# Output projection on scaled fp16 weight parts, in one pipeline with the feed-forward stage

## The chip, the core and the metric

The kernel runs on one core of a Trainium2 chip. The metric is the device time of one execution in microseconds; lower is better. The engines of the core are named as in the profile: PE (TensorE, matmuls) with PEld (its weight loads), DVE (VectorE), ACT (ScalarE), POOL (GpSimd) and SP (SyncE, which here only issues DMAs).

## What is computed

One step of a decoder layer for 288 token rows: a prompt of 256 tokens and 8 samples of 4 tokens each. All inputs are fp32. The parts that matter here are the end of the mixer, the output projection and the feed-forward network:

```
mod = silu(c) @ w_ada + b_ada                  # sh1, sc1, gt1, sh2, sc2, gt2, 2048 each
gate   = sigmoid(mg).reshape(B, T, 3, 2048)    # mg is a part of xn @ w_in
merged = gate[:, :, 0] * (y_lru @ w_br_lru) + gate[:, :, 1] * (y_gla @ w_br_gla) + gate[:, :, 2] * (y_ml @ w_br_ml)
x  = x + gt1 * (merged @ w_out)                # w_out 2048 x 2048
xn = rmsnorm(x, g_norm2) * (1.0 + sc2) + sh2
x  = x + gt2 * (square(relu(xn @ w_ff1)) @ w_ff2)   # w_ff1 2048 x 8192
y  = rmsnorm(x, g_final)
```

Everything before `merged` (three recurrent branches and their states) is computed by the kernel as well and is the same on both sides of the change.

## The kernel before

Activations lie with features on the 128 partitions and the 288 tokens along the free axis; a row of 2048 features is 16 such tiles, called k = 0 to 15 below. Weights stream from memory in tiles of 128 x 1024 values (0.5 MB). To keep fp32 accuracy each weight and each activation is split into a high and a low part, and each product is three matmuls: high by high, high by low, low by high. A step is one weight tile: 24 matmuls of 128 x 128 by 288.

There are two such streams. `stream` (L152) does the input projection, the gates, the branch projections and the output projection: ACT writes the high part of a tile as fp32r (L160), DVE the low part (L162), and the matmuls follow at L169. It has three buffers each for the raw tile, the high and the low part. The feed-forward stage uses `Block` (L226): it first finds a power of two for the whole block of four tiles (`scan`, a sum of squares on ACT, L236; `total`, one small matmul with a tile of ones, L240; `scale`, a few one-column DVE operations, L195), and then splits the scaled tile into fp16 parts (`convert`, L249 on ACT or L251 on DVE for the high part, L252 on DVE for the low part). The matmuls are at L263. `feed_forward` (L1956) is a list of 256 steps; in step s it converts tile s + 3, fetches tile s + 14, scans tile s + 10 and multiplies tile s. A block of w_ff1 is 256 columns wide with four k in a tile, a block of w_ff2 512 columns with two k in a tile.

Order is set in four ways. Under `in_order` (L207) the instructions of PE, ACT and DVE are issued as they stand in the program. `tc.issue_after` ties single instructions behind another. The rest of PE, ACT, DVE and POOL is ordered by the compiler's scheduler, with `tc.high_priority` for hints. SP alone issues strictly in the program's order, and a DMA whose target is still in use holds all those behind it.

Beside the main stream runs the conditioning product (mod). Its weights come in loads of 1 MB. A string of letters after `every(` says what is done after each step: L loads one unit, V multiplies all loaded units, F four of them, C advances the splitting of a unit that is multiplied in fp16 parts (`cond_parts`, L403; its matmuls are at L433), and a dot does nothing. Units without parts (`cond_product`, L355) are multiplied in plain fp32 at L372. The order of the units is fixed in `units` (L527). The second half of SC2 (the units sm1) is multiplied in parts beside the output projection; the eight units of the first half of GT2 (gt0) are loaded then too and are multiplied at its end.

Around the change the work runs like this. `merge` (L1295) is called for each of the three branches; for each of four blocks of 512 columns it runs eight steps of a gate block (w_in), then four steps of the branch block. In the third call POOL adds the last term (L1330) and ACT and DVE split the merged rows into fp32r parts (L1333, L1334), which lie in slots 0 to 3. Slots are ten buffers of 128 x 8 x 288 fp32 that are used in turn. The gates read the normalised input from two larger tiles, xh and xl, which are free after the last gate block. The output projection (L1780 on) is 4 blocks of 8 steps with `ev_o` as eviction: residual (`resid`, L1763), squares for the norm (`sumsq`, L593). In its last block the rows are scaled by SC2 on POOL (`scaled`, L1773). After it come the row sums with ones (L608), the root (`rstd_of`, L636), and `second_norm` (L1815), which makes the fp16 parts of the normalised row k: a product by the root (L1820, DVE, or POOL for every fourth k), the high part with the shift on ACT (L1821, the samples at L1824), the low part on DVE (L1825, samples L1826). The first four feed-forward steps each begin with four of these, and their matmuls go through the k one by one.

## Time and profile before

| | us |
|---|---|
| median of 3 runs | 1898.62 |
| lowest, highest run | 1896.01, 1898.95 |
| the profiled execution, whole | 1895.68 |
| its span in the profile | 1893.9 |
| granted clock over the span | 0.995 |

A line of a timeline has the start and length in us, the engine, the line of the kernel, the operation, what it writes and reads, and in brackets how long the engine sat idle before it and what ended that. A line by stretch has, after the stretch and its length, the busy time and the number of instructions of PE, PEld, DVE, ACT and POOL, the granted clock of PE, the busy share of the DMA engines and the rate. A line of waits has the waiting engine and its line, the engine and line that ended the wait, the total in us, how often, and the longest. Ends of matmuls are modelled, so their pace is read from starts and counts.

### The profile page before, as it was taken

To read this page: it belongs to the slowest core of one execution; us is meant where nothing else is said; L and a number is where in the kernel's file an instruction comes from. 1 tells how busy PE (TensorE), PEld (TensorE's weight loads), DVE (VectorE), ACT (ScalarE), POOL (GpSimd) and SP (SyncE) were. 2 spreads that over 40 slices of the span, in tenths; PEclk is the share of its full clock that TensorE was granted. 3 is DMA by queue.
4 is the path that set the end of the run, shared out by engine and by line. 5 is a ranking of instruction groups with operands and counts; after the bars stand their busy time and mean duration, and the time that the engine had idled before them with its cause. 6 is when DMAs were issued, how large, how long until landed. Compare 5 with 4: busy or idle time off the path is not lost.

```text
span 1893.9 us, 38893 instructions
## 1 busy us (share of the span) xinstructions
PE 1847.8 (98%) x15874; PEld 1621.6 (86%) x15874; DVE 1268.2 (67%) x2239; ACT 1117.3 (59%) x1861; POOL 219.9 (12%) x302
## 2 busy tenths in 40 slices
PE   8999999999999999999999979999999999999997
PEld 7998889999999999999999947777777777777775
DVE  4767846645684557776558678776868676767676
ACT  5333374545454444566448568877777766666673
POOL 0001200000123010011101520000000000000091
PEclk9999999999999999999999999999999999999999
DMA  9998666547844358856787656565556555556541
GB/s 384 398 372 301 242 236 240 201 145 260 276 159 168 134 172 296 302 204 223 296 341 298 246 210 222 172 222 185 189 188 203 176 181 168 188 169 188 168 155 51
DMA packets 113442, 422.90 MB, mean 223 GB/s; under 512 B 11808, under 2 KB 12096, under 8 KB 110064
## 3 DMA queue, kind: packets, MB, share of 16 engines
q1 hardware_dynamic: 97040, 361.04, 54.9%
q0 software_dynamic: 11472, 42.79, 6.4%
q10 hardware_dynamic: 4752, 16.60, 2.2%
q8 instruction: 124, 2.03, 0.4%
q14 instruction: 54, 0.44, 0.1%
HBM read 403.56 MB, written 16.81 MB: 222 GB/s over the span
## 4 chain that ended last, share of the span: by engine, by line
PE 80%; DVE 9%; ACT 6%; issue 3%; DMA 1%; POOL 0%; SPq 0%; DVEq 0%; ACTq 0%; POOLq 0%
PE mm L169 39%; PE mm L263 24%; PE pi L263 6%; PE pa L372 3%; DVE pair L252 2%; ACT pair L249 2%; PE px L169 2%; DVE lo L162 1%; ACT con L236 1%; DMA raw<-win 1%; ACT hi L160 1%; PE pa L433 1%; DVE pair L251 0%; DVE s L800 0%; PE px L1649 0%
## 5 line engine op out<-in xcount | busy, mean ns | idle before, releaser
L263 PEld LDWEIGHTS <-pair 128*128 128x128 f16 x6144 | 596.6, 98 | 176.8 <-issue 11.9
L160 ACT ACTIVATE hi<-raw 128x1024 fp32r<-128x1024 f32 x272 | 286.9, 1057 | 407.4 <-PE mm L169 250.4
L162 DVE TENSOR_TENSOR lo<-raw,hi 128x1024 fp32r<-128x1024 f32 x272 | 334.9, 1233 | 248.0 <-ACT hi L160 227.9
L169 PE MATMUL mm<-xh,hi 128*128 128x288 f32 x1440 | 429.4, 301 | 4.0 <-ACT xh L718 1.7
L169 PE MATMUL mm<-xl,hi 128*128 128x288 f32 x1440 | 423.5, 297 | 0.0
L169 PE MATMUL mm<-xh,lo 128*128 128x288 f32 x1440 | 411.9, 296 | 2.0 <-DVE lo L162 1.9
L263 PE MATMUL mm<-x,pair 128*128 128x288 f16 x2448 | 316.1, 287 | 10.1 <-ACT x L1824 6.3
L263 PE MATMUL mm<-hx,pair 128*128 128x288 f16 x2472 | 321.8, 286 | 2.7 <-ACT s L1873 1.4
L169 PEld LDWEIGHTS mm<-xh,hi 128*128 128x128 f32 x1440 | 270.4, 188 | 15.8 <-issue 8.1
L169 PEld LDWEIGHTS mm<-xl,hi 128*128 128x128 f32 x1440 | 270.8, 188 | 1.4
L169 PEld LDWEIGHTS mm<-xh,lo 128*128 128x128 f32 x1440 | 266.0, 188 | 4.9 <-DVE lo L162 2.9
L169 PE MATMUL mm<-s,hi 128*128 128x288 f32 x1280 | 252.8, 297 | 1.1 <-DVE s L1769 0.7
L169 PEld LDWEIGHTS mm<-s,hi 128*128 128x128 f32 x1280 | 201.8, 188 | 5.1 <-issue 2.9
L169 PE MATMUL mm<-s,lo 128*128 128x288 f32 x640 | 179.2, 296 | 1.6 <-DVE lo L162 1.0
L252 DVE SCALAR_TENSOR_TENSOR pair<-xl,sums,pair 128x1024 f16<-128x1024 f32 x92 | 117.8, 1284 | 62.9 <-ACT pair L249 61.6
L252 DVE SCALAR_TENSOR_TENSOR pair<-s,sums,pair 128x1024 f16<-128x1024 f32 x92 | 118.1, 1284 | 52.7 <-ACT pair L249 51.4
L252 DVE SCALAR_TENSOR_TENSOR pair<-raw,sums,pair 128x1024 f16<-128x1024 f32 x72 | 93.2, 1295 | 41.6 <-ACT pair L249 40.6
L169 PEld LDWEIGHTS mm<-s,lo 128*128 128x128 f32 x640 | 116.9, 188 | 2.3 <-DVE lo L162 2.1
L1861 POOL TENSOR_SCALAR s<-s,mod 128x256 f32<-128x256 f32 x16 | 21.5, 1347 | 675.7 <-DVE s L1877 675.7
L236 ACT ACTIVATE con<-s 128x1024 bf16<-128x1024 f32 x92 | 96.3, 1046 | 1.3 <-DMA s<-wf 0.3
L236 ACT ACTIVATE con<-xl 128x1024 bf16<-128x1024 f32 x92 | 96.2, 1046 | 0.9
L263 PE MATMUL pi<-hx,pair 128*128 128x288 f16 x600 | 89.8, 286 | 3.1 <-DVE rs_t L1767 1.8
(526 smaller groups left out, 2275.7 us busy)
## 6 DMA issues: line engine op xcount, KB each, us to landing
raw<-win SPq DMA_DIRECT2D x192, 512.0 KB, 4.4
s<-wf SPq DMA_DIRECT2D x92, 512.0 KB, 3.9
xl<-wf SPq DMA_DIRECT2D x92, 512.0 KB, 4.1
raw<-wf SPq DMA_DIRECT2D x72, 512.0 KB, 3.9
s<-wq SPq DMA_DIRECT2D x20, 1024.0 KB, 8.7
raw<-wout SPq DMA_DIRECT2D x32, 512.0 KB, 5.9
s<-wada SPq DMA_DIRECT2D x13, 1024.0 KB, 7.3
ag<-wada POOLq DMA_DIRECT2D x12, 1024.0 KB, 7.8
```

Of the source, the lines that this page charges most:

```text
L160: pace["hi"] = S.activation(hi, raw, AF.Copy)
L162: pace["lo"] = V.tensor_tensor(out=lo, in0=raw, in1=hi.bitcast(F32), op=ALU.subtract)
L169: pace["last"] = T.matmul(ps, w[:, kk, ms], x, start=k == k0 and i == 0, stop=k == kt - 1 and i == 2)
L236: pace["hi"] = S.activation(junk, raw, AF.Square, accum_out=self.of[:, g:g + 1])
L249: pace["hi"] = S.activation(hi, raw, AF.Copy, scale=self.u)
L252: pace["lo"] = V.scalar_tensor_tensor(lo, raw, self.u, hi, ALU.mult, ALU.subtract)
L263: pace["last"] = T.matmul(self.ps[m][:, :N], a[:, kk, m * P:(m + 1) * P], x, start=k == 0 and i == 0, stop=k == 4 * self.kg - 1 and i == 2)
L372: pace["prod"] = T.matmul(ps[32 * j:32 * j + 32, h * w // 4:(h + 1) * w // 4], stat(k), v[:, j], start=k == 0 and h == 0, stop=k == kt - 1 ...
L433: pace["prod"] = T.matmul(ps[32 * j:32 * j + 32, a:a + 256], c, v[:, j], start=q == i == n == 0, stop=q == KT // each - 1 and n == 1, skip ...
L1861: G.tensor_scalar(a[:, 0:NP], a[:, 0:NP], mod[:, GT2, k, 0:1], None, ALU.mult)
```

## The change

The output projection leaves `stream` and becomes eight `Block`s of 256 columns (w_out is packed for that width) at the front of one list with the feed-forward blocks. The list is driven by `feed`, and a record `pipe` holds the state: which tiles are fetched, scanned, converted. A tile is fetched as soon as a place is free, scanned two steps after its fetch at the earliest and up to 12 ahead, and converted up to 5 ahead.

The merged rows become fp16 parts as well. Their power of two must be known before the last rows are there, so it is taken from a bound: the squares of the sums so far, of the last branch weights (`weigh`) and of the norm's weights (`whole_bound`). `halve_merged` then writes the parts, k 0 to 3 in the last branch block and 4 to 15 ahead of the first three projection steps.

The ramp of the pipeline lies in the last part of the third `merge` call. Behind the first step of its third branch block six tiles of w_out are fetched into slots 2, 3 and 5 (`fetch_first`); they are scanned in the last gate block (`gate_then`). Behind the first step of the last branch block four more are fetched into xl, and behind that block three into the raw buffers.

The first two feed-forward blocks are joint: a step takes tile g of both, 48 matmuls, and each of the four steps begins with four `second_norm`s. The units sm1 are no longer in parts; the letter W multiplies one unit. The row sums for the norm are all made at the last k.

The diff, cut to its core:

```diff
+            if on_raw:
+                on_raw(g, flat(raw))
...
+            if then:
+                then(g)
             yield
...
+    def pipe_scan(to):
+        while pipe["scanned"] <= to and pipe["when"].get(pipe["scanned"], pipe["time"]) <= pipe["time"] - 2:
+            i = pipe["scanned"]
+            pipe["blocks"][i // 4].scan(i % 4, pipe["raws"][i])
...
+    def nth(n):
+        j = n - pipe["joint"]
+        return pipe["joint"] + j // 2 + 4 * (j % 2) if 0 <= j < 8 else n
+
+    def pipe_convert(to, rate=2):
+        pipe_scale()
+        for n in range(pipe["converted"], min(to + 1, pipe["converted"] + rate)):
+            i = nth(n)
+            if i // 4 >= pipe["scaled"]:
+                break
...
+            t = wp.tile([P, 2048], F16, tag=("hi", "lo")[n % 2], name=nm("pair"), bufs=3)
...
+            if all(raw is not o for o in pipe["once"]):
+                pipe["places"].append(raw)
+            pipe["converted"] += 1
+            pipe_fetch()
...
+    def feed(count, act, evac, back, factor=1.0, joint=False, late=False):
+        if joint:
+            s = pipe["at"]
+            two = pipe["blocks"][s // 4:s // 4 + 2]
+            for g in range(4):
+                pipe["time"] += 2
+                with in_order():
+                    with ahead():
+                        for f in pipe["before"].pop(s + g, ()):
+                            f()
+                        for b in two if g == 0 else ():
+                            b.start(act, back() if callable(back) else back, factor)
+                        pipe_convert(s + 2 * g + 5)
+                        pipe_scan(s + min(2 * g + 12, 15))
+                    for kk in range(two[0].kg):
+                        for i, b in enumerate(two):
+                            b.multiply(g, *pipe["pairs"][s + 4 * i + g], range(b.nm_t), (kk,))
...
-            yield from ada_half(f"sm{h}", SC2, h, h == 1)
+            yield from ada_half(f"sm{h}", SC2, h)
...
+    pipe["blocks"] += [Block(io["wout"], i, 256) for i in range(8)]
+    for hb in range(9):
+        if hb < 8:
+            pipe["blocks"] += [Block(io["wf1"], 4 * hb + i, 256, by_act=(0,)) for i in range(4)]
+        if hb:
+            pipe["blocks"] += [Block(io["wf2"], i, 512, g0=4 * (hb - 1), by_act=(0, 2, 3)) for i in range(4)]
...
+    def fetch_first():
+        once = [v for i in (2, 3, 5) for v in views(flat(slot(i)))]
+        pipe["once"] = once
+        pipe["places"] += once
+        pipe["time"] += 1
+        with behind_last():
+            pipe_fetch()
...
+    def whole_bound():
+        p = rows_total(zof, 14)
+        for a, b, o in ((0, 8, 14), (8, 12, 15), (12, 14, 4)):
+            V.tensor_reduce(out=zof[:, o:o + 1], in_=p[:, a:b], axis=AX.X, op=ALU.add)
...
+        roots_of(zof)
+        for k in range(4):
+            halve_merged(k)
+
+    def halve_merged(k):
+        m, a, u = mrg[k // 8], acc[k // 8][:, k % 8, :], zof[:, 6:7]
+        S.activation(m[:, 0, k % 8], a, AF.Copy, scale=u)
+        V.scalar_tensor_tensor(m[:, 1, k % 8], a, u, m[:, 0, k % 8], ALU.mult, ALU.subtract)
+
+    def outs_then(g):
+        pipe["time"] += 1
+        with behind_last():
+            if g == 0:
+                bigx.append(flat(big.tile([P, KT, N], F32, tag="xl", name=nm("xl"))))
+                pipe["places"] += views(bigx[0], 4)
+                pipe_fetch()
...
-            run(stream(w, b, lambda k: (y[0][:, k, :], y[1][:, k, :]), 8, ev))
+            ramp = {"on_raw": weigh, "then": outs_then} if br == 2 and b == 3 else {"then": lambda g: fetch_first() if g == 0 else None} if br == 2 and b == 2 else {}
+            run(stream(w, b, lambda k: (y[0][:, k, :], y[1][:, k, :]), 8, ev, **ramp))
...
-    every("L L . L CC CC CC CC CC CC . V . . . L L L CC CC CC CC CC CC V" + 3 * " . . . L L L V", skip=4)
+    every("L L . L CC CC CC CC CC CC . V . . . L L L CC CC CC CC CC CC V S" + 4 * " . L L . V", skip=4)
...
-    every("L L . L CC LCC CC LCC CC LCC CC LCC F LCC CC LCC CC LCC CC LCC CC LF . . L L . L L . . ." + 20 * " .")
+    every("L L . . LW . . LW . . LW . . LW . . LW . . LW . . LW . . LW . . W L L . L . . . ." + 20 * " .")
...
+    raw3 = [wp.tile([P, 1024], F32, tag="raw", name=nm("raw"), bufs=3) for _ in range(3)]
+    pipe["places"] += raw3
+    with in_order(), ahead():
+        pipe_fetch()
+        pipe_convert(1)
+        pipe_convert(3)
+    for g in range(1, 4):
+        pipe["before"].setdefault(g - 1, []).extend([lambda k=k: halve_merged(k) for k in range(4 * g, 4 * g + 4)])
...
-        run(stream(io["wout"], b, act_m, KT, ev_o))
+    run(feed(6, act_m, ev_o, zof[:, 5:6], 0.5))
+    drain("sm1")
...
+    run(feed(2, act_m, lambda m, p, c: ev_o(12 + m, p, c), zof[:, 5:6], 0.5, late=True))
...
-    run(feed_forward())
+            run(feed(4, lambda k: (x16[:, 0, k, :], x16[:, 1, k, :]), ev_1(hb), xback, joint=hb == 0))
...
-        "wout": pack(I["w_out"][0]), "wf1": pack(I["w_ff1"][0], 256), "wf2": pack(I["w_ff2"][0]),
+        "wout": pack(I["w_out"][0], 256), "wf1": pack(I["w_ff1"][0], 256), "wf2": pack(I["w_ff2"][0]),
```

More of the change, by code (lines that the diff above doesn't have):

```diff
@@ L78, in slot @@
     def slot(i, dt=F32):
[L79 removed]
+        shape = [P, 2, 8, N] if dt == F16 else [P, 8, N]
+        return big.tile(shape, dt, tag=f"s{i}", name=nm(f"s{i}"))
     def flat(t):
@@ L202, in power_of_two, with rows_total @@
         return t, u
+    def power_of_two(p, n, of):
+        V.tensor_reduce(out=of[:, 4:5], in_=p[:, 0:n], axis=AX.X, op=ALU.add)
+        return roots_of(of)
+    def rows_total(of, n):
+        p = misc()
+        T.matmul(p[:, 0:n], words(ones, 1, BF16), words(of[:, 0:n], 1, BF16), start=True, stop=True)
+        return p
     queued = {}
@@ L264, in multiply, with pipe_fetch @@
                                                 stop=k == 4 * self.kg - 1 and i == 2)
+    pipe = {"blocks": [], "places": [], "raws": {}, "pairs": {}, "fetched": 0, "scanned": 0, "converted": 0, "totals": 0, "scaled": 0, "at": 0,
+            "time": 0, "when": {}, "seen": {}, "before": {}, "after": {}, "once": (), "joint": 32}
+    def pipe_fetch():
+        while pipe["places"] and pipe["fetched"] < 4 * len(pipe["blocks"]):
+            i = pipe["fetched"]
+            b, raw = pipe["blocks"][i // 4], pipe["places"].pop(0)
+            Q.dma_start(raw, b.w[b.blk, b.g0 + i % 4])
+            pipe["raws"][i] = raw
+            pipe["when"][i] = pipe["time"]
+            pipe["fetched"] += 1
@@ new lines, in ev_o @@
+    def ev_o(k, p, c):
+        if k % 2 == 0:
+            g = mod[:, GT1, k:k + 2, :]
+            V.tensor_scalar(g, g, c, None, ALU.mult)
+        x = x2[k // 8][:, k % 8, :]
+        resid(x, p, GT1, k)
+        if k == KT - 1:
+            with tc.high_priority(), tc.issue_after(pace["last"].ins):
+                visit(2)
+            with tc.issue_after(pace["prod"].ins):
+                sumsq(pss, x, k, ssum)
+            with tc.high_priority(), tc.issue_after(pace["sum"].ins):
+                visit()
+        else:
+            sumsq(pss, x, k, ssum)
+        if k == KT - 4:
+            S.activation(sc([P, 1], "warm", 1), ssum[:, 0:1], AF.Sqrt)
@@ new lines, in trunk @@
+    run(feed(6, act_m, ev_o, zof[:, 5:6], 0.5))
+    drain("sm1")
+    xof = sc([P, 8], "xs", 1)
+    for i, (kind, f) in enumerate(((SC2, 64.0), (SH2, 2.0))):
+        S.activation(t288()[:, 0:9 * KT], modf[:, 9 * KT * kind:9 * KT * (kind + 1)], AF.Square, scale=f, accum_out=xof[:, i:i + 1])
+    p = misc()
+    T.matmul(p[:, 0:2], ones, xof[:, 0:2], start=True, stop=True)
+    xback, u = power_of_two(p, 2, xof)
+    r = modf[:, 9 * KT * SH2:9 * KT * (SC2 + 1)]
+    V.tensor_scalar(r, r, u, None, ALU.mult)
@@ L1811, in trunk @@
+    xf.extend((slot(6), slot(7)))
+    for i in range(3):
+        scaled(i)
+    run(feed(2, act_m, lambda m, p, c: ev_o(12 + m, p, c), zof[:, 5:6], 0.5, late=True))
     every("")
@@ new lines, in trunk @@
+    big8, big3 = flat(slot(8)), flat(slot(3))
+    pipe["places"] += [t[:, 1024 * i:1024 * i + 1024] for t in (big8, big3) for i in range(2)]
+    assert pipe["joint"] == pipe["at"]
+    taken.update(of=5, n=0)
+    scaled(3)
+    rs = rstd_of(pss)
+    s0 = pipe["at"]
+    for i in range(4):
+        pipe["before"][s0 + i] = [lambda k=k: second_norm(k) for k in range(4 * i, 4 * i + 4)]
+    slots.update(ids=(9, None, "st"), n=0)
+    every("E L . . L . . L . . C . . C . . C . . C . . C . . C . . C . . C . . C . . C . . C . . C . V . .")
@@ L1987, in trunk @@
-    with in_order():
-        for i in range(4):
-            fetch(i)
-        for i in range(4):
-            scan(i)
-        for i in range(4, 12):
-            fetch(i)
-        blocks[0].total()
-        blocks[0].scale()
-        convert(0)
-    scaled(3)
-    rs = rstd_of(pss)
-    slots.update(ids=(9, None, "st"), n=0)
-    high.update(ids=(None,))
-    every("E L . . L . . L . . C . . C . . C . . C . . C . . C . . C . . C . . C . . C . . C . . C . V . .")
-    run(feed_forward())
+            run(feed(4, lambda k: (x16[:, 0, k, :], x16[:, 1, k, :]), ev_1(hb), xback, joint=hb == 0))
```

353 lines of the change are left out of this document (172 added, 181 removed).

## The prediction

> **What bounds the kernel now.** I read the page first, then the busy time by stretch, PE's waits, and the timelines of PE, SP, ACT and DVE around the output projection.
>
> ```profile
> span 1893.9 us, 38893 instructions
> PE 1847.8 (98%) x15874; PEld 1621.6 (86%) x15874; DVE 1268.2 (67%) x2239; ACT 1117.3 (59%) x1861; POOL 219.9 (12%) x302
> PE 80%; DVE 9%; ACT 6%; issue 3%; DMA 1%; POOL 0%; SPq 0%; DVEq 0%; ACTq 0%; POOLq 0%
> ...
> L160 ACT ACTIVATE hi<-raw 128x1024 fp32r<-128x1024 f32 x272 | 286.9, 1057 | 407.4 <-PE mm L169 250.4
> L162 DVE TENSOR_TENSOR lo<-raw,hi 128x1024 fp32r<-128x1024 f32 x272 | 334.9, 1233 | 248.0 <-ACT hi L160 227.9
> ```
>
> TensorE is the bound: only its own time and its gaps count, and work taken from other engines pays only where PE waits for it. The last two lines are the halves into which every fp32 weight tile is split, 1.06 us on ACT and 1.23 on DVE. By stretch (columns: length; busy and instructions of PE, weight loads, DVE, ACT, POOL; granted clock; DMA share; GB/s):
>
> ```profile
> 932.00:952.00 20.00, 20.00 (x152) 20.00 (x152) 7.40 (x7) 6.37 (x6) 0.00 (x0) 1.00 0.82 309
> 1150.00:1190.00 40.00, 40.00 (x332) 32.01 (x330) 31.67 (x58) 32.72 (x65) 0.00 (x0) 1.00 0.57 184
> 973.63:1084.70 111.07, 108.39 (x903) 105.46 (x899) 81.03 (x155) 78.69 (x122) 31.40 (x29) 1.00 0.79 300
> 1092.53:1135.66 43.13, 31.28 (x218) 20.23 (x209) 30.50 (x60) 29.37 (x67) 12.34 (x31) 0.92 0.55 205
> 1103.00:1106.50 3.50, 3.34 (x14) 1.96 (x14) 2.79 (x5) 3.08 (x7) 1.59 (x5) 0.51 0.94 372
> ```
>
> A split-fp32 matmul takes 20.00/152 = 131.6 ns, an fp16 one 40.00/332 = 120.5 ns. The third line is the whole output projection, 111.1 us. The fourth runs from the first normalised row to the end of the first two feed-forward blocks: 43.1 us for 192 matmuls, 23.1 us of work. The stall there, by PE's waits:
>
> ```profile
> PE mm L263 <- ACT x L1824: 6.3, 8, 2.0
> ```
>
> It waits for the second normalisation, channel by channel. Its borders on PE:
>
> ```profile
> 973.63 0.53 PE L169 MATMUL mm<-s,hi 128*128 128x288 f32 x2
> ...
> 1084.70 1.93 PE L372 MATMUL pa<-xh,silc 128*32 128x256 f32 x32
> 1086.45 1.91 PE L372 MATMUL pa<-s,silc 128*32 128x256 f32 x32
> 1088.29 0.18 PE L240 MATMUL px<-sums,ones 128*128 128x4 bf16 x1
> 1088.33 0.73 PE L608 MATMUL pi<-row,ones 128*128 128x288 f32 x2
> ...
> 1089.96 1.93 PE L372 MATMUL pa<-xl,silc 128*32 128x256 f32 x32
> ...
> 1135.66 1.51 PE L263 MATMUL pi<-x,pair 128*128 128x288 f16 x11
> ```
>
> Between the projection's last matmul and the normalisation, the eight loads of the first half of GT2 fill PE; the row sums (L608) are a fifth of that.
>
> **Part one: the joint blocks.** DVE sets the pace of the normalisation:
>
> ```profile
> 1092.53 0.46 DVE L1820 TENSOR_TENSOR row<-s,row 128x288 f32<-128x288 f32 x1
> ...
> 1099.85 0.45 DVE L1820 TENSOR_TENSOR row<-s,row 128x288 f32<-128x288 f32 x1
> 1100.88 0.48 DVE L1825 SCALAR_TENSOR_TENSOR x<-row,mod,x 128x256 f16<-128x256 f32 x1 [0.58 <-ACT x L1821]
> ...
> 1104.91 0.75 DVE L251 TENSOR_SCALAR pair<-raw,sums 128x1024 f16<-128x1024 f32 x1
> 1105.69 1.28 DVE L252 SCALAR_TENSOR_TENSOR pair<-raw,sums,pair 128x1024 f16<-128x1024 f32 x1
> 1106.90 0.45 DVE L1820 TENSOR_TENSOR row<-s,row 128x288 f32<-128x288 f32 x1
> ```
>
> Four channels take 1104.91 − 1099.85 = 5.06 us (in each, DVE waits 0.58 us for ACT's half), and one converted weight 1106.90 − 1104.91 = 1.99 us. The function is unchanged and the order is still fixed, so that pace stays. Blocks of w_ff1 convert tile 0 with ACT's help and the rest on DVE alone. In the new order three pairs are ready when the joint steps begin; by the rate and the rule that a block must be scaled first, two, two and one conversions stand between the four normalisation groups: 4 × 5.06 + 5 × 1.99 = 30.2 us to the last channel, one more for the ACT scans that are bunched in the second joint step, 2.0 for the last channel's twelve matmuls (12 × 0.12 = 1.4) behind its last half, and 0.7 for the scale and the low half of the block after. That is 33.9 against 43.1: **−9.2 us**. PE's 23.1 us of work now lie almost wholly under it. Bounds: −17 if DVE's order overlaps better, so that PE's work and a start of 3 us remain, −6 if the clock falls.
>
> **Part two: from the last projection matmul to the first normalised row.** Before, 1092.53 − 1084.70 = 7.8 us. One GT2 load costs (1088.29 − 1084.70)/4 = 0.90 us of PE. Following the load letters through, four loads of GT2 are left unvisited at the end of the projection, two are visited inside it and two after the last matmul: 1.8 us, then the sums 1089.96 − 1088.33 = 1.6 us, then the same root and transposes, 1092.53 − 1089.96 = 2.6 us, and 0.3 us for the late conversions ahead of them on DVE: 6.3. **−1.5 us** (−3 to 0). But the four loads that no longer fill this wait are done inside the feed-forward stage, where PE has nothing to spare: 4 × 0.90 = **+3.6 us** (2 if small stalls there take some of them in, 3.7 if none does).
>
> **Part three: the projection itself.** SC2's second half loses its fp16 parts. What these cost on PE:
>
> ```profile
> 903.53 0.29 PE L433 MATMUL pa<-uh,uc 128*32 128x256 f16 x4
> ...
> 904.96 0.40 PE L169 MATMUL mm<-xh,hi 128*128 128x288 f32 x1
> ```
>
> Three loads in 904.96 − 903.53 = 1.43 us, 0.48 each. Before: 768 × 131.6 ns = 101.1, plus 8 × 0.48 = 3.8, is 104.9 of the 111.1 us; 6.2 were lost to ACT and DVE. After: 768 × 120.5 ns = 92.5, plus ten plain loads (eight of SC2, two of GT2) at 0.90 = 9.0. In steady state a step of 24 matmuls (2.9 us) asks of ACT one scan and three quarters of a conversion, of DVE a low half and half a residual: some 2 us each, so the stalls go. The ramp puts one in. Rows for ACT's pieces:
>
> ```profile
> 902.78 2.05 ACT L160 ACTIVATE hi<-raw 128x1024 fp32r<-128x1024 f32 x2
> ...
> 928.82 0.90 ACT L1333 ACTIVATE s<-s 128x288 fp32r<-128x288 f32 x2
> ...
> 1104.43 1.04 ACT L236 ACTIVATE con<-s 128x1024 bf16<-128x1024 f32 x1
> ...
> 1105.60 1.06 ACT L236 ACTIVATE con<-s 128x1024 bf16<-128x1024 f32 x1
> ```
>
> The merged rows can be scaled only after the bound over all of them, so between that scale and the fourth step ACT has in its queue 16 copies at 0.45 (7.2), six conversions at 1.0 (6.0) and five scans at 1.17 (5.9): 19.1 us; then DVE's last half (0.45) and 15 matmuls (1.8) make 21.4. The row sum behind the scale can go ahead of the last branch step's 3.2 us, and eight small DVE operations follow it; I estimate the scale to be known 2.5 us before the last branch matmul. From there 2.5 us of branch work, two waiting loads (1.8) and four steps (4 × 24 × 0.1205 = 11.6) keep PE busy for 16.0 us. **Stall 5.4 us** (2 to 12; behind the scans on ACT queue the conversions, behind those DVE's halves, and PE waits for all three). The stage: 92.5 + 9.0 + 5.4 = 106.9 against 111.1, **−4.2 us**.
>
> **Part four: the prefetch on SP's queue.** SP issues in program order, and its waits hold everything behind:
>
> ```profile
> 900.20 0.33 SPq L159 DMA_DIRECT2D raw<-win  x1
> 903.30 0.33 SPq L159 DMA_DIRECT2D raw<-wbm  x1
> 904.20 1.01 SPq L485 DMA_DIRECT2D ag<-wada  x1
> 905.76 0.33 SPq L159 DMA_DIRECT2D raw<-wbm  x1
> ...
> 942.48 6.62 SPq L159 DMA_DIRECT2D raw<-wbm  x3
> ...
> 959.07 0.38 SPq L485 DMA_DIRECT2D xh<-wada  x1
> ```
> ```profile
> 912.11 1.06 ACT L160 ACTIVATE hi<-raw 128x1024 fp32r<-128x1024 f32 x1 [2.72 <-DMA raw<-wbm]
> ```
> ```profile
> DMA to landing us min/median/max: 3.3/5.1/10.0
> ```
> ```profile
> 965.00:975.00 10.00, 10.00 (x94) 8.91 (x93) 5.90 (x10) 3.48 (x6) 3.51 (x4) 1.00 1.03 420
> ```
>
> The last line is the rate when the queue is full, 420 GB/s; a branch weight (0.52 MB) lands in 3.3 us at best, 2.0 of it fixed. The gate's xh tile is free when its last matmul ends, and the load into it goes out at 959.07, that moment.
>
> Six w_out tiles (3.15 MB) now go out behind the first weight of branch block 2 and ahead of its second, and the conditioning load of the step before comes ahead too: from 904.20 on, 1.05 + 0.52 + 3.15 + 1.05 + 0.52 = 6.3 MB up to that second weight. At 420 GB/s plus 2.0 us it lands at 921.2 (before, its conversion began at 912.11); with 1.06 for the high half PE can start at 922.3, and at 923.5, after 1.23 more, it has the low half that all but two of the step's 24 matmuls stand behind. PE wants the tile at 904.96 + four steps of 24 × 0.1316 = 3.2 us, at 917.8, and would be done with the step at 921.0; it is done at 923.5 + 22 × 0.1316 = 926.4, 5.4 us late. By the slower landing of the row at 905.76 (6.3 us with little ahead) it would be 7. Then four more tiles go into xl, free at about 959, between the first and the second weight of branch block 3, which before went out with the x3 at 942.48. The second weight is issued at about 960.5 behind 2.1 MB and lands 8.5 us after the gate's end; with both halves it is ready at 10.8, its step over at 13.7. Without a wait PE would have done a step, two loads that are now visited there, and this step, 3.2 + 1.8 + 3.2 = 8.2: again 5.5, or 7. I take **6 us each** (2 to 8, nearest to the row of the landing at its best). Load letters now come every five steps and use one buffer (ag) that the visit two steps before frees, so the weights behind them have two steps of lead in place of four: **+2 us** (0 to 3).
>
> An idle stretch costs more than itself here: the line of 1103 to 1106.5 has the clock granted at 0.51, after the thin stretch of the normalisation. Half speed for 3.5 us costs 1.7; I take one of the two stalls to be followed by it: **+1.7 us** (0 to 3.4).
>
> [...]
>
> POOL's work (scaling by SC2, the sums) stays in its order and far from late; the x loads stay on ACT's queue. The feed-forward stage keeps 120.5 ns; its small stalls stay.
>
> **Sum.** 12 + 2 + 1.7 − 4.2 − 1.5 − 9.2 + 3.6 = **+4.4 us**. The profiled execution took 1895.68 (span 1893.9), so it would take 1900.1; it lies 2.9 below the median of the three runs, 1898.62, so I predict a median of **1903.0**. A measurement of this kernel can tell about 0.2% (3.8 us) from no change.
>
> **Rivals.** *The prefetch hides* (faster, 1887): the weights behind it arrive in time, because the scheduler's SP order or the fill of the queue differs from my reading. For it: PE had no wait at all in this stretch before, with the queue already at 420 GB/s. Against: 959.07 shows SP waiting for a tile. It decides if the second weight lands within some 10 us of the row at 904.20. Without 12 + 2 + 1.7 the sum is −11.3. *The joint steps run at PE's pace* (about 1895): −17 in place of −9.2 gives −3.4. Against: DVE's row with its 0.58 us wait. *The ramp costs 12* (1910): ACT's 19.1 us start only at the end of the branch, because the scale chain lies behind the block's own evictions on DVE; +6.6 gives +11.0. For it: ACT and DVE are both near full in that list. That the change does not do what it says, no joint gain since the same serial DVE order stays, would need the conversions to grow by as much as they did, and is the upper end of the range.
>
> **Chances.** Forecast 0.48 (own range 1898 to 1908), hidden prefetch 0.24, joint at PE's pace 0.13, long ramp 0.15. Faster by over 0.2% (below 1894.8): 0.02 + 0.20 + 0.05 = 0.27. Slower (above 1902.4): 0.27 + 0.14 + 0.01 = 0.42. Within: 0.31. The range, from the hidden prefetch to the long ramp, is 1886 to 1912.
>
> **What would show it.** Right: PE waits for DVE's low half of a branch weight (raw<-wbm) twice, 5 to 7 us each, at the second weight of the last two branch blocks; a third wait for scaled merged rows in the first four projection steps; projection matmuls at 120.5 ns; the joint steps some 33 us with DVE near full; ag loads inside the first feed-forward blocks. Wrong: PE full through the last branch blocks, or a joint stretch near 25 us.

## The result and the profile after

The changed kernel is slower: a median of 1919.01 us (four runs, 1917.11 to 1921.15) against 1897.32 us (four runs, 1895.53 to 1898.95), a ratio of 1.0115 with a 95% interval of 1.0097 to 1.0132. The forecast, 1903.0, had the direction, but 1919.0 lies above its range, 1886 to 1912. The profiled execution of the changed kernel took 1921.15 us; its span is 25.4 us longer than that of the kernel before.

The page's head, to be read beside the one shown in the prediction:

```profile
span 1919.3 us, 38963 instructions
PE 1856.1 (97%) x15883; PEld 1602.5 (83%) x15883; DVE 1255.1 (65%) x2238; ACT 1120.2 (58%) x1877; POOL 208.9 (11%) x302
```

TensorE is busy for 8 us more and idle for 17 us more. Busy time rose although 768 matmuls became cheaper, and the granted clock over the span is 0.987 where it was 0.995, which already points to stretches at half clock. The stretches of the changed kernel, in the columns explained above: branch block 2 of the third merge, its last gate block, its last branch block, the projection, the rows up to the end of the first two feed-forward blocks, and the rest.

```profile
914.40:937.75 23.35, 17.20 (x130) 15.87 (x129) 6.26 (x7) 4.66 (x5) 1.59 (x2) 0.85 0.58 223
937.75:969.94 32.19, 29.36 (x228) 26.80 (x227) 10.72 (x14) 20.89 (x38) 1.62 (x3) 1.00 0.59 232
969.94:996.67 26.73, 20.24 (x164) 17.32 (x163) 7.82 (x18) 12.93 (x25) 2.87 (x4) 0.87 0.81 315
996.67:1117.25 120.58, 109.58 (x926) 80.14 (x928) 74.34 (x160) 73.95 (x121) 25.46 (x31) 0.96 0.65 234
1117.25:1159.40 42.15, 33.65 (x250) 23.18 (x250) 31.18 (x64) 22.84 (x55) 13.90 (x33) 0.88 0.47 163
1159.40:1919.00 759.60, 745.32 (x6232) 592.13 (x6230) 554.13 (x968) 539.04 (x955) 55.91 (x59) 0.99 0.55 183
```

The first three of them in the kernel before, in the same view (its projection was shown):

```profile
914.66:930.26 15.60, 15.60 (x147) 14.16 (x145) 8.25 (x11) 6.71 (x9) 4.49 (x4) 1.00 0.67 241
930.26:958.88 28.62, 28.62 (x245) 27.18 (x241) 10.36 (x11) 9.11 (x11) 0.73 (x1) 1.00 0.76 284
958.88:973.63 14.75, 14.75 (x130) 13.66 (x128) 6.40 (x9) 4.53 (x7) 2.92 (x4) 1.00 1.02 418
```

Before, PE is full in all three. After, the first has 6 us of idle time and a clock of 0.85, the second 3 us of idle time, the third 6.5 us and a clock of 0.87. With the projection ending at 1084.70 and the joint part at 1135.66 before, the 25.4 us are, stretch by stretch:

| stretch | before | after | difference | forecast |
|---|---|---|---|---|
| up to branch block 2 | 914.66 | 914.40 | −0.3 | 0 |
| branch block 2 | 15.60 | 23.35 | +7.8 | |
| last gate block | 28.62 | 32.19 | +3.6 | |
| last branch block, to the projection | 14.75 | 26.73 | +12.0 | these three: +15.7 |
| projection | 111.07 | 120.58 | +9.5 | −4.2 |
| to the end of the first two feed-forward blocks | 50.96 | 42.15 | −8.8 | −10.7 |
| rest | 758.24 | 759.90 | +1.7 | +3.6 |

The gain of the joint blocks came nearly as forecast. Two stretches went wrong: the one ahead of the projection by 7.6 us, and the projection itself by 13.7. TensorE's waits name the places (columns: who waits for whom, us in total, times, longest):

```profile
PE mm L172 <- ACT hi L161: 14.9, 4, 6.2
PE px L216 <- ACT con L250: 9.5, 4, 5.3
PE mm L278 <- ACT x L2060: 7.7, 3, 3.5
```

The first line is the late branch weights that the prediction asks for, twice 6 us, and 1.4 and 1.3 us. The third is the normalisation. The second, a block's total waiting for squares on ACT, is in no step of the prediction. Its place on PE, beside the two late weights and the first stall of the ramp:

```profile
923.95 2.29 PE L172 MATMUL mm<-s,hi 128*128 128x288 f32 x8 [6.15 <-ACT hi L161]
...
981.18 2.29 PE L172 MATMUL mm<-s,hi 128*128 128x288 f32 x8 [6.02 <-ACT hi L161]
...
1000.13 4.66 PE L278 MATMUL mm<-s,pair 128*128 128x288 f16 x23 [3.04 <-DVE pair L263]
...
1112.10 0.17 PE L216 MATMUL px<-sums,ones 128*128 128x4 bf16 x1 [5.33 <-ACT con L250]
```

Behind each of the long waits the clock is halved (the clock is the third number from the end of a line):

```profile
920.00:921.79 1.79, 0.00 (x0) 0.00 (x0) 0.00 (x0) 0.00 (x0) 0.00 (x0) 1.00 1.00 407
921.81:928.62 6.81, 4.67 (x19) 4.67 (x20) 3.67 (x3) 3.18 (x3) 0.00 (x0) 0.50 0.46 173
...
1112.00:1117.20 5.20, 5.10 (x25) 3.19 (x24) 1.23 (x4) 0.50 (x2) 0.94 (x1) 0.58 0.01 3
```

PE works at half speed for 4.68 us behind the first wait, for 5.47 behind the second (981.18 to 986.65) and for 4.26 behind the third (1112.10 to 1116.36). Each wait thus costs 2.1 to 2.7 us more than its bracket says.

Why the weights were late is read from SP's queue and from ACT, which splits them:

```profile
903.97 0.38 SPq L619 DMA_DIRECT2D ag<-wada  x1
904.44 0.42 SPq L160 DMA_DIRECT2D raw<-wbm  x1
904.91 3.12 SPq L289 DMA_DIRECT2D s<-wout  x6
908.98 1.55 SPq L619 DMA_DIRECT2D st<-wada  x2
911.48 2.80 SPq L160 DMA_DIRECT2D raw<-wbm  x3
...
956.73 0.41 SPq L160 DMA_DIRECT2D raw<-wbm  x1
970.00 1.76 SPq L289 DMA_DIRECT2D xl<-wout  x4
972.17 0.81 SPq L160 DMA_DIRECT2D raw<-wbm  x2
```
```profile
922.84 1.06 ACT L161 ACTIVATE hi<-raw 128x1024 fp32r<-128x1024 f32 x1 [7.79 <-DMA raw<-wbm]
...
980.07 1.06 ACT L161 ACTIVATE hi<-raw 128x1024 fp32r<-128x1024 f32 x1 [8.50 <-DMA raw<-wbm]
```

The order is the predicted one. From the ag load on, 6.3 MB come down in 922.84 − 903.97 = 18.9 us up to the second branch weight, 333 GB/s. In the last block SP issues nothing between 957 and 970.00, when the gate's last matmul (969.94) frees xl.

### The profile page after: what moved, and what is told of

Same layout as the page of the kernel before. It is cut to its first block, busy times and chain, and to the rows that moved or that the text cites. A ratio compares the mean times of both kernels' runs of the same rounds, so it can differ in the third digit from the quotient of the medians.

```text
span 1919.3 us, 38963 instructions
## 1 busy us (share of the span) xinstructions
PE 1856.1 (97%) x15883; PEld 1602.5 (83%) x15883; DVE 1255.1 (65%) x2238; ACT 1120.2 (58%) x1877; POOL 208.9 (11%) x302
## 5 line engine op out<-in xcount | busy, mean ns | idle before, releaser
L278 PEld LDWEIGHTS <-pair 128*128 128x128 f16 x6912 | 674.5, 98 | 204.7 <-issue 18.6
L161 ACT ACTIVATE hi<-raw 128x1024 fp32r<-128x1024 f32 x240 | 253.9, 1059 | 402.6 <-PE mm L172 241.3
L163 DVE TENSOR_TENSOR lo<-raw,hi 128x1024 fp32r<-128x1024 f32 x240 | 295.9, 1234 | 254.7 <-ACT hi L161 233.6
L263 DVE SCALAR_TENSOR_TENSOR pair<-xl,sums,pair 128x1024 f16<-128x1024 f32 x109 | 140.7, 1290 | 56.6 <-ACT pair L260 54.8
L172 PE MATMUL mm<-s,hi 128*128 128x288 f32 x768 | 157.6, 303 | 12.2 <-ACT hi L161 12.2
L172 PEld LDWEIGHTS mm<-s,hi 128*128 128x128 f32 x768 | 125.3, 193 | 16.0 <-ACT hi L161 12.9
L250 ACT ACTIVATE con<-xl 128x1024 bf16<-128x1024 f32 x109 | 114.3, 1048 | 24.4 <-issue 13.0
L250 ACT ACTIVATE con<-s 128x1024 bf16<-128x1024 f32 x98 | 102.8, 1049 | 20.3 <-issue 17.3
L172 PE MATMUL mm<-s,lo 128*128 128x288 f32 x384 | 111.4, 300 | 0.0
L278 PE MATMUL mm<-s,pair 128*128 128x288 f16 x768 | 100.8, 293 | 4.7 <-DVE pair L263 3.0
L260 ACT ACTIVATE pair<-xl,sums 128x1024 f16<-128x1024 f32 x55 | 63.0, 1146 | 55.0 <-PE mm L278 30.5
L250 ACT ACTIVATE con<-raw 128x1024 bf16<-128x1024 f32 x81 | 84.9, 1048 | 16.4 <-issue 6.9
```

The lines of the kernel that those rows point to most:

```text
L161: pace["hi"] = S.activation(hi, raw, AF.Copy)
L163: pace["lo"] = V.tensor_tensor(out=lo, in0=raw, in1=hi.bitcast(F32), op=ALU.subtract)
L172: pace["last"] = T.matmul(ps, w[:, kk, ms], x, start=k == k0 and i == 0, stop=k == kt - 1 and i == 2)
L250: pace["hi"] = S.activation(junk, raw, AF.Square, accum_out=self.of[:, g:g + 1])
L260: pace["hi"] = S.activation(hi, raw, AF.Copy, scale=self.u)
L263: pace["lo"] = V.scalar_tensor_tensor(lo, raw, self.u, hi, ALU.mult, ALU.subtract)
```

## Experiments

Single runs of one kernel scatter by some 2 us to either side of their median (the changed kernel's four runs do), so small effects are read from the stretches and only larger ones from the times. Each edit by itself (e1 to e7) has one run. Its time stands against the changed kernel's median, 1919.0, and its stretches against the profiled execution of that kernel, which took 1921.15, so that a saving read from stretches comes out some 2 us larger; ratios are to the kernel before, timed on the same chip, whose median was 1895.8 to 1897.3 us each time. The edits are shown as they change the code after.

**The three waits, one by one.** First the xl weights, behind two more branch weights:

```diff
 def outs_then(g):
-            if g == 0:
+            if g == 2:
                 bigx.append(...); pipe["places"] += views(bigx[0], 4); pipe_fetch()
+                pipe["when"].update({i: pipe["time"] - 1 for i in range(6, 10)})
...
-            pipe_scan((5, 5, 7, 7)[g])
+            pipe_scan((5, 5, 5, 7)[g])
             if g == 3:
+                pipe["time"] += 1
                 pipe_total(1)
```

> The four output-projection weights that go into the xl tiles are fetched after step 2 of the last branch block instead of after step 0, behind the second and third weight of the block on SP instead of ahead of them. Theory (order on SP: the four wait for the gate block's last matmul at 969.94, and the block's second weight waits behind them and behind their 2 MB): TensorE's wait of 6.02 us at the block's second step and the half clock after it (5.32 us for 22 matmul records, about 2.4 us lost) go, at most 2 us come back at the fourth step, and the run takes 1912 us (1910.5 to 1914) where the changed kernel takes 1919. Rival (the queue's bytes, not their order: the same weights are due by the start of the projection, so what is not waited for here is waited for in the ramp): the wait moves to the fourth step or to the first three projection steps, whose stall grows from 6.8 to 12 us or more; 1918 to 1920 us.

Measured: 1916.9 us, between the two, so that the time alone decides nothing. The wait of 6.02 us at the second step is gone. But SP shows what stands behind the four now, and ACT and PE what that costs:

```profile
971.22 1.79 SPq L289 DMA_DIRECT2D xl<-wout  x4
977.68 0.38 SPq L619 DMA_DIRECT2D ag<-wada  x1
978.17 0.84 SPq L160 DMA_DIRECT2D raw<-wbm  x1
```
```profile
984.03 1.06 ACT L161 ACTIVATE hi<-raw 128x1024 fp32r<-128x1024 f32 x1 [6.97 <-DMA raw<-wbm]
```
```profile
993.58 0.16 PE L216 MATMUL px<-sums,ones 128*128 128x4 bf16 x1 [3.65 <-ACT con L250]
```

The block's fourth weight, behind the xl weights and behind an ag load that waits for its own buffer, lands late, and the squares of two xl weights, which stand behind it on ACT, come late too. The last branch block takes 23.0 us up to the projection, and the projection 118.0: better by 3.7 and 2.6 us, while the gate block ahead happened to end 1.7 us later. So the mechanism is order on SP, but this edit moves half of the wait on.

The first six weights the same way:

```diff
-            ... {"then": lambda g: fetch_first() if g == 0 else None} ...
+            ... {"then": lambda g: fetch_first() if g == 3 else None} ...
```

> The first six output-projection weights are fetched after step 3 of branch block 2 instead of after step 0, behind all four weights of that block on SP. Theory (order on SP): TensorE's wait of 6.15 us at the block's second step and the half clock after it (about 2 us) go; the next gate block's first weight, now behind the six, still lands before it is due some 10 us later; the run takes 1911 us (1909.5 to 1913.5). Rival (bytes): the same wait of about 6 us appears at the first or second step of gate block 3, which stands behind the six now; 1918 to 1920 us.

Measured: 1910.8 us, as the theory had it. Branch block 2 by stretch:

```profile
913.80:928.63 14.83, 14.83 (x130) 13.73 (x129) 5.12 (x7) 4.15 (x5) 1.59 (x2) 1.00 0.91 348
```

PE is full at full clock, where the changed kernel needed 23.35 us; the last gate block shows no new wait (31.0 us against 32.2), and of its two waits for a weight one of 1.3 us is left. The same bytes at another place in the queue cost nothing here.

Then the instruction ahead of the squares on ACT. What the changed kernel's ACT and POOL did there:

```profile
1100.21 1.28 ACT L2031 ACT_TABLE_LOAD   x1
1109.29 0.20 ACT L2031 ACTIVATE warm<-row 128x1 f32<-128x1 f32 x1 [7.80 <-POOL row L735]
...
1109.73 1.04 ACT L250 ACTIVATE con<-raw 128x1024 bf16<-128x1024 f32 x1
```
```profile
1094.18 3.64 POOL L2011 TENSOR_SCALAR s<-s,mod 128x256 f32<-128x256 f32 x4 [6.86 <-DVE mod L2042]
...
1108.47 0.78 POOL L735 TENSOR_TENSOR row<-row,t 128x288 f32<-128x288 f32 x1
```

The warm-up root reads the sum of squares of k = 12. That sum is one POOL operation of 0.78 us, behind 14.3 us of the scaling by SC2. While ACT waits for it, the squares of the block's last weights (L250) wait behind it, and PE waits for the block's total.

```diff
-            S.activation(sc([P, 1], "warm", 1), ssum[:, 0:1], AF.Sqrt)
+            S.activation(sc([P, 1], "warm", 1), eps[:, 0:1], AF.Sqrt)
```

> The early square root on ScalarE, there only to load the activation table, reads a constant column instead of the sum of squares that GpSimd writes. Theory (that instruction waits 7.8 us for a sum which stands behind the scaling on GpSimd, and the squares of the last four projection weights stand behind it on ScalarE): TensorE's wait of 5.33 us for the block's total at 1112.1 and the half clock after it (24 matmuls in 5.16 us where a step takes 3.0) go; the run takes 1911.6 us (1910.5 to 1913). Rival (the squares are late because the feed-forward weights that they read land late): the wait stays within 1 us of 5.33, ended by a DMA on ScalarE; 1918 to 1920 us.

Measured: 1912.0 us. ACT goes straight through:

```profile
1097.03 1.28 ACT L2031 ACT_TABLE_LOAD   x1
1098.32 0.20 ACT L2031 ACTIVATE warm<-eps 128x1 f32<-128x1 f32 x1
```

The wait at the total is gone, and the projection takes 111.4 us instead of 120.6. The rival falls. All three together:

> The three edits together. Theory (three waits, each with its own half clock, independent of each other): the savings add up, 7.0 + 8.0 + 7.4 = 22.4, so 1896.6 us (1894 to 1900), a ratio to the kernel before of 0.998 to 1.001. Rival (the two SP edits hand their waits on to the ramp or to each other): 1903 to 1911 us, with a longer stall in the first three projection steps or in gate block 3.

Measured: 1901.31 us (ratio 1.0022, interval 1.0012 to 1.0031). Single savings of 2.2, 8.2 and 7.0 make 17.4; together they save 17.7. As far as single runs can show it, they add up, and the shortfall against the 22.4 expected is nearly all the xl edit's.

**Order or bytes.** The ten fetches, called at the same places of the program, but issued by GpSimd:

```diff
-    def pipe_fetch():
+    def pipe_fetch(q=Q):
...
-            Q.dma_start(raw, b.w[b.blk, b.g0 + i % 4])
+            q.dma_start(raw, b.w[b.blk, b.g0 + i % 4])
...
+    pipe_fetch(G)        # in fetch_first and at the xl tiles in outs_then
```

> The changed kernel with the ten early projection weights fetched at the same two places, but issued by GpSimd and not by SP; bytes, buffers and due times are the same, and nothing on SP stands behind them. Theory (order on SP: the block's second weight stands behind transfers that wait for a buffer, and behind their bytes): both waits at the second step (6.15 and 6.02 us) with their half clocks go, or leave at most 2 us each; 1904 us (1902 to 1907.5). Rival (bytes: the 16 DMA engines are full and the second weight is late whoever issues the ten): waits of 3 to 6 us stay at both places; 1911 to 1919 us.

Measured: 1908.9 us, 1.4 above the theory's bound and below all of the rival's. But the edit did more than change the queue. Of the first six weights four went out some 80 to 90 us earlier (two of them are shown), and only two at about the old place (907.01):

```profile
825.28 1.05 POOL L289 DMA_DIRECT2D s<-wout  x2 [8.65 <-PE px L1181]
```

The waits left at the two places (two of 1.3 us in the last gate block are left too):

```profile
919.50 1.32 PE L172 MATMUL mm<-s,hi 128*128 128x288 f32 x8 [0.63 <-ACT hi L161]
...
978.40 1.31 PE L172 MATMUL mm<-s,hi 128*128 128x288 f32 x8 [0.92 <-ACT hi L161]
```

At the second place all four xl weights still go out when the gate block ends (964.51), while on SP the block's next weights had gone out from 950.89 on, before that. There it was order on SP: the weights had been held behind transfers that waited for their buffer. At the first place this edit can't part order from bytes, since 1.05 MB went out there and not 3.15; the test for that place is e2, where the six go out together, behind the due weights, and cost nothing. Whether all six on a queue of their own would have delayed the due weight is not shown. The last branch block takes 21.1 us up to the projection. The gain is smaller than the waits that went: at the projection's start PE now waits 2.5 us and, two matmuls later, 2.2 us for converted pairs, which the late weights had covered.

**The rhythm of the conditioning loads.** Three loads every seven steps, as before the change, with two uh tiles in the place of slot 5:

```diff
-    also["S"] = lambda: slots.update(ids=(None, "st"), n=0)
+    also["S"] = lambda: slots.update(ids=(None, "st", "uh"), n=0)
-    every("... V S" + 4 * " . L L . V", skip=4)
+    every("... V S" + 3 * " . . . L L L V", skip=4)
```

> The changed kernel with the rhythm of before in the last merge: three conditioning loads together every seven steps (ag, st and, in place of slot 5, two uh tiles), instead of two every five. Theory (lost lead: an ag load every five steps keeps the gate weights behind it on SP): gate block 3, which took 32.2 us, goes back towards 28.5, its two waits of 1.44 and 1.28 us for a weight go, and the run takes 1915 us (1913.5 to 1917) where the changed kernel takes 1919. Rival (those waits are what the six early projection weights leave behind, whatever the rhythm of the small loads): both waits stay, 1918 to 1921 us.

Measured: 1913.5 us, but in good part for another reason than I gave. The two waits in the last gate block go; its length stays 32.2 us, since it now multiplies six loads of 0.9 us instead of two. Most of the gain comes from branch block 2, which takes 13.6 us (no load is multiplied in it) and has no wait at its second weight, though the six still go out ahead of it:

```profile
902.71 4.54 SPq L289 DMA_DIRECT2D s<-wout  x6
907.35 0.44 SPq L160 DMA_DIRECT2D raw<-wbm  x1
```
```profile
917.23 1.06 ACT L161 ACTIVATE hi<-raw 128x1024 fp32r<-128x1024 f32 x1 [0.59 <-DMA raw<-wbm]
```

With the letters elsewhere no conditioning load is among them: 4.2 MB instead of 6.3 in front of (and with) that weight, so its conversion starts 5.6 us earlier, at 917.23. (The block itself starts 1.6 us later in this run, at 916.03, which helps.) That is the same cause as in the edits before, bytes ahead on one queue, in a third way. The projection starts at 986.37, 10.3 us earlier, but the span is only 7.7 us shorter: from the last projection matmul on it is 3.0 us longer. The projection itself takes 120.2 us as against 120.5, though the wait behind the warm-up root grew from 5.3 to 7.0 us.

**The joint blocks undone.**

```diff
-        return pipe["joint"] + j // 2 + 4 * (j % 2) if 0 <= j < 8 else n
+        return n
...
-            run(feed(4, ..., ev_1(hb), xback, joint=hb == 0))
+            run(feed(4, ..., ev_1(hb), xback, joint=False))
```

> The changed kernel with the first two feed-forward blocks one after the other, as in the kernel before, and not joint. Theory (joint blocks halve how often TensorE has to wait for the next four normalised rows): the stretch from the last projection matmul to the end of these two blocks grows by about 8 us, so 1927 us (1925 to 1929). Rival (VectorE's normalisation sets the pace of this stretch either way): 1918 to 1921 us.

Measured: 1926.1 us, 7 above the changed kernel. From the last projection matmul to the end of the second block it takes 48.7 us, against 42.1: the joint order is worth 6.5 us there. The edit also takes the matmuls of these steps one column tile after the other and not k by k, as the kernel before did; what that costs is in the 6.5. One cost of the joint order shows beside it. In the changed kernel ACT has four evictions in a row at the end of the joint steps, the squares come late, and PE waits 2.7 us at a block's total:

```profile
1177.00 0.16 PE L216 MATMUL px<-sums,ones 128*128 128x4 bf16 x1 [2.74 <-ACT con L250]
```

Without the joint order that wait is absent, but the one behind the warm-up root is longer (9.56 us at 1113.99); why is open.

**The ramp by itself.**

```diff
 def gate_then(g):
-                squares_of(i, acc[i // 4][:, 2 * (i % 4):2 * (i % 4) + 2], 1.0)
+                for k in (2 * g - 4, 2 * g - 3):
+                    halve_merged(k)
...
-    ramp = {"on_raw": weigh, "then": outs_then} ...
+    ramp = {"then": outs_then} ...
-    for g in range(1, 4):
-        pipe["before"]...extend([... halve_merged(k) for k in range(4 * g, 4 * g + 4)])
+    pipe["before"].setdefault(2, []).extend([... halve_merged(k) for k in range(12, 16)])
+    V.memset(zof[:, 5:7], 1.0)
```

> The changed kernel with the bound left out: the merged rows are scaled by the constant 1 and not by a power of two worked out from them and from the last branch block's weights (their squares and totals are not computed), so that twelve of the sixteen rows are halved inside the last gate block and only four in front of the projection's fourth step. Theory (the ramp's stall is the halving of 16 rows between the first conversions): the first three steps, which took 15.6 us, come down to 9 to 10, and the run takes 1912.5 us (1910.5 to 1914.5) where the changed kernel takes 1919. Rival (the ramp is paced by the conversion of the first weights, on ScalarE and VectorE): the first three steps stay above 13 us; 1917 to 1920 us.

Measured: 1914.7 us, 0.2 above the theory's bound. The first three projection steps take 1006.47 − 996.84 = 9.6 us where they took 15.6, with one wait left:

```profile
997.88 8.75 PE L278 MATMUL mm<-s,pair 128*128 128x288 f16 x70 [0.63 <-DVE pair L263]
```

So the bound, with the halving that waits for it, is the ramp's stall, 6 us of it. The edit takes away the squares and totals of the bound and moves the halving ahead, both at once; how the 6 us are shared between them is not shown. The whole projection went from 120.6 to 113.9.

**Combinations.** All four edits to order, with the six later on SP and the xl weights on GpSimd:

> The constant under the early square root, the first six weights fetched after step 3, the four xl weights issued by GpSimd, and three loads every seven steps, together. Theory (each wait has its own cause): 1901.3 us of the three edits together, less about 5 us for what the xl weights still cost there (waits of 0.95, 1.34 and 3.66 us between 976 and 987), less about 4 us for the lead: 1892 us (1889 to 1896), a ratio to before of 0.996 to 1.000. Rival (what the edits save in the last merge is given back in the ramp, as the xl edit did): 1898 to 1903 us.

Measured: 1898.33 us (ratio 1.0013, interval 1.0004 to 1.0023), inside the rival's range and outside the theory's. The projection starts at 977.15, 19.5 us earlier than in the changed kernel, but takes 113.7 us, with nearly the ramp of the changed kernel (14.7 us for the first three steps) and a wait of 2.69 us at 1067.83 for a conditioning load. Without the rhythm:

> The three edits with the xl weights issued by GpSimd at their old place, and the rhythm of the conditioning loads left as the change has it. Theory (the xl weights on SP still cost some 3.5 us: with them on GpSimd the last branch block took 21.1 us to the projection's start, with them later on SP 24.6): 1897.8 us (1895 to 1900). Rival (the lead is what is missing, so only the rhythm helps): 1900 to 1903 us.

Measured: 1899.32 us (ratio 1.0016, interval 1.0006 to 1.0026), as the theory had it. By the medians the xl weights on GpSimd are worth 2 us more than later on SP, and the rhythm 1 us on top of that; these intervals resolve neither. The same with the bound left out and a constant scale:

> The kernel before this one in the list, with the bound left out and twelve rows halved in the last gate block (the scale is the constant 1). Theory (the ramp's stall stands alone, behind nothing else): 7 us below the other, 1890.8 us (1888 to 1894), a ratio to before of 0.995 to 0.998. Rival (what the ramp no longer waits for, the next conversions wait for): 1895 to 1900 us.

Measured: 1894.12 us (ratio 0.9983, interval 0.9973 to 0.9992). This is 5.2 us below the kernel before it in this list (b2) where the theory said 7, and 0.1 us above the theory's range: the ramp stands alone, but a wait of 2.25 us for the first pair remains. The projection takes 107.0 us. And with the rhythm as well:

> The kernel with the three edits, the xl weights on GpSimd and the bound left out (1894.1 us), and the rhythm of three conditioning loads every seven steps on top. Theory (the lead and the ramp are separate terms, and the rhythm's own worth is what it gave the four edits with the bound kept, about 1 us): 1893 us (1890.5 to 1895), a ratio to before of 0.997 to 0.9985. Rival (the three-load rhythm moves its gain into later waits for conditioning loads, as the wait of 2.69 us at 1067.8 showed): 1894 to 1898 us.

Measured: 1891.61 us (ratio 0.9975, interval 0.9966 to 0.9983), the fastest of all, 4.2 us below the kernel before, with the bound left out. The rhythm gave 2.5 us here by the medians; the two intervals overlap. With the constant nothing fits the scale to the size of the merged rows, so the last two kernels tell what the bound costs and don't take the changed kernel's place.

## Why the prediction was off

**Late weights behind the prefetch, 6 us each.** Right in place, cause and size: 6.15 and 6.02 us at the second weight of the last two branch blocks. The first goes when the six stand behind the due weights (e2), the second when the xl weights leave SP (e5). The releaser on PE was ACT's high half, not DVE's low half: eight matmuls of the step, and not two, went ahead of the low half (x8 at 923.95). The 2.0 us that the step counts as fixed in a landing are an estimate, 3.3 us less 0.52 MB at 420 GB/s (1.2 us); no run shows them by themselves. Measured, the 6.3 MB took 18.9 us up to the high half, where the step has 921.2 − 904.20 = 17.0.

**Half clock after one of the two, 1.7.** Undersized. Both waits are followed by it, with 4.68 us of work at half speed after the first and 5.47 after the second: 2.3 and 2.7 us.

**Lost lead, +2.** Right within 1 us: 1.44 and 1.28 us of waits in the last gate block, gone with the old rhythm (e3). One of the two also goes when the six are fetched later (e2), so the rhythm is not the only cause. The same letters also put 2.1 of the 6.3 MB in front of the first late weight; the prediction counts them there, but did not see that the old rhythm alone would have removed that wait. Waits, half clocks and lead make 12.2 + 5.1 + 2.7 = 20.0 of the 23.0 us lost ahead of the projection; 0.5 is the wait at its start, and the other 2.5 are not put down to single places.

**The projection, −4.2.** Here the prediction failed. The step that failed reads: "POOL's work (scaling by SC2, the sums) stays in its order and far from late". It did stay in its order, but the blocks became half as wide. Row k = 12 is now evicted some 17 us before the projection's end, and its sum lands behind the scaling on POOL, which holds it up to 1108.47. In the kernel before, the last four rows are evicted together at the projection's end; the sum stood behind some of the scaling too, but it was done at 1086.50, before ACT had loaded its table (up to 1087.45), and ACT did not wait:

```profile
1085.70 0.80 POOL L601 TENSOR_TENSOR row<-row,t 128x288 f32<-128x288 f32 x1
```
```profile
1087.46 0.20 ACT L1795 ACTIVATE warm<-row 128x1 f32<-128x1 f32 x1
```

ACT's warm-up root reads that sum. The wait and its half clock cost 7.0 us by the time of e4, 9.2 by its stretch. The wait can't be seen in the trace of before; it could have been found by asking, for every instruction on ACT in this stretch, what it reads, and who writes that now.

The ramp's stall, 5.4, was 6.8 by the trace and 6.0 by the edit (e7): right in place, a little small (the sum has 16.0 us where its own terms make 15.9), and on DVE's pairs more than on ACT. With both of them gone (b3) the stage takes 107.0 us, which is nearly the forecast that counts 5.4 for the ramp; so the forecast's plain part, 101.5, was some 3 us short. Most of that is two readings. The price of an fp16 matmul, 120.5 ns, came from 332 records in 40.00 us, which also count the matmuls of the totals and those that the window cuts. By starts it is higher, in the kernel before already:

```profile
1171.15 8.98 PE L263 MATMUL mm<-x,pair 128*128 128x288 f16 x72
```

The next instruction starts at 1179.97, so 72 matmuls take 8.82 us, 122.5 ns each, and 768 of them 94.1 us, not 92.5. In the changed projection they keep that pace. A plain load takes 1.00 us there (1018.25 to 1019.25), not 0.90: ten of them are another 1.0 us. By starts a split-fp32 matmul takes 133.3 ns and not 131.6, so the gain per matmul, 10.8 ns, is nearly the forecast 11.1.

**From the last projection matmul to the first normalised row, −1.5.** 6.9 us where 6.3 was forecast, with three loads visited there and not two.

**The joint blocks, −9.2.** Right in kind. From the first normalised row to the end of the two blocks it takes 35.3 us, forecast 33.9, before 43.1; DVE's serial pace sets it: DVE is busy for 25.9 of the 35.3 us and still waits 0.58 us for ACT's half in most rows. Undone by itself the joint order is worth 6.5 us in that stretch (e6). It hands 2.7 us back at 1177.00, and a half clock behind it (3.41 us from 1177.80), both of which the prediction missed: ACT catches up with four evictions.

**Loads inside the feed-forward stage, +3.6.** Only 1.7 us show there, and 2.7 of the wait just named is in them. Small stalls that the prediction left in place vanished. From 1200 to 1800 us PE is busy for 600.00 us in the changed kernel and for 595.83 in the kernel before, both at full clock. Most of the 4.2 us of idle time before were waits for the evictions of the second feed-forward product (L1873 on ACT, L1877 on DVE); why they are gone is not settled, and no run tests it.

**The rivals.** The prefetch did not hide, the joint steps did not run at PE's pace, and the ramp did not cost 12. The case that happened, a second engine's wait inside the projection, was none of them. Without it (e4) the time is 1912.0, the upper end of the range; the rest of the miss is the second half clock and the short breaks ahead of the projection.

Why the change as a whole brought no gain: the cheaper fp16 matmuls (768 × 10.8 ns, some 8 us) and the joint blocks (6.5 us) are real, but the waits that their prefetch, load rhythm, warm-up and ramp make (23.0, 7.0 and 6.0 us) cost more than twice as much. The mended order (b1) gives back 20.7 of the 21.7 us, and only without the bound's ramp (b3, b4) does the scheme come out ahead.

## What to carry to other kernels

The prefetch cost here what stood behind it on its queue: with 6.3 MB from the ag load on, at 333 GB/s, PE waited 6.15 us for a due weight, and with the six tiles behind the last due weight (e2) that wait was gone; the xl weights cost 6.02 us on SP and 0.92 on a queue of their own (e5). So add the bytes between a due weight and the one before it, and divide by the rate that the queue has in the trace; then move the prefetch behind the last weight that is due, or to a queue that nothing due shares. When a stage's block size changes, go through every small instruction that rides on its evictions and ask which queue its operand is written on and what is ahead of it there: one sum of 0.78 us on POOL, behind 14.3 us of scaling, cost 7.0 us (e4). Charge a long wait with its half clock too: behind the waits of 6.15, 6.02 and 5.33 us it cost 2.1 to 2.7 us more each.

## What the runs showed of the hardware

From 900 us on, PE has seven waits of over 2 us in the changed kernel, and up to 1911 us its trace has seven stretches with a granted clock of 0.50, one at each of them:

| PE's wait, us | its end | half clock from | for, us |
|---|---|---|---|
| 6.15 | 923.95 | 921.80 | 6.83 |
| 6.02 | 981.18 | 979.83 | 6.83 |
| 3.04 | 1000.13 | 1000.31 | 3.41 |
| 5.33 | 1112.10 | 1109.53 | 6.83 |
| 3.53 | 1125.33 | 1126.60 | 3.41 |
| 2.92 | 1144.52 | 1143.66 | 6.83 |
| 2.74 | 1177.00 | 1177.80 | 3.41 |

Each begins inside its wait or at most 1.27 us behind its end. The length of a wait alone does not tell whether one follows. The third wait in the normalisation has the same length in two kernels, 2.92 us in the changed kernel and 2.91 in e1. In the changed kernel, then in e1:

```profile
1140.25:1143.65 3.40, 1.34 (x11) 0.93 (x10) 2.69 (x4) 3.31 (x7) 0.24 (x1) 1.00 0.50 155
1143.67:1150.48 6.81, 5.86 (x24) 3.44 (x24) 4.80 (x9) 3.73 (x12) 3.45 (x8) 0.50 0.61 229
```
```profile
1138.47:1141.87 3.40, 1.59 (x12) 1.15 (x12) 1.44 (x4) 2.21 (x6) 1.95 (x5) 1.00 0.76 274
1141.89:1145.29 3.40, 3.14 (x26) 2.31 (x24) 2.68 (x6) 2.23 (x7) 1.72 (x5) 1.00 0.63 251
```

In the changed kernel PE is busy for only 1.34 of the 3.40 us ahead of the half clock, and then 5.86 us of busy time lie at a clock of 0.50, which is 2.9 us lost. In e1 the two lines have 1.59 and 3.14 us of work, and the clock stays at 1.00. What makes the difference is not shown. So the same short wait was followed by a loss of 2.9 us in one kernel and of none in the other, and a single run can't resolve edits of that size.
